# The last layer's residual: transposed by DMA during the layer in place of TensorE in the closing

## The chip, the cores and the metric

One Trainium2 chip; the kernel runs on one of its cores. The metric is device time in microseconds (us), as a median of several runs. A profile is one more execution with the hardware profiler on. It tells for each instruction when it ran and for each DMA when it landed. PE is TensorE, DVE VectorE, ACT ScalarE, POOL GpSimd, and SP the engine that here only issues DMAs. Each engine works off its own list of instructions in order, and waits where an instruction's inputs or its room are not ready.

## The reference

A trunk of two layers on 1024 tokens of 1024 channels: one layer with gated linear attention, one with chunked attention, each followed by a gated feed-forward part, and a last norm over the channels. What matters here is the end of the last layer:

```python
def conv_ffn(xn, w_up, conv_w, conv_b, w_down):
    h = causal_dwconv(xn @ w_up, conv_w) + conv_b
    gate, val = h[..., :FFN_DIM], h[..., FFN_DIM:]
    return (jax.nn.silu(gate) * val) @ w_down
...
        h = h + conv_ffn(rmsnorm(h, f_norm[layer]), f_w_up[layer], f_conv[layer], f_conv_b[layer], f_w_down[layer])
    return rmsnorm(h, final_norm)
```

All arrays are float32, and FFN_DIM is 2816. The `h` ahead of the plus sign is the residual.

## The kernel before

Activations lie with channels on the 128 partitions and tokens along the free dimension, until the last layer's end. The output wants tokens on the partitions: eight token tiles of 128 x 1024.

Every product is made of three matmuls, since each float32 operand is split in a high and a low part (`triple`). ScalarE makes the high part (a cast, L1434), GpSimd or VectorE the low part (a subtraction, L1412).

`ffn` (L1407) is the feed-forward part, called once for each layer. Its work is a list of steps, `seq`, in TensorE's order; a step is twelve matmuls of 512 columns, some 2.7 us. Beside it, `at(i, f, rank)` hangs work of the other engines on a step: in the loop at the function's end all jobs of step i are issued by rank, and then the step's matmuls. So `at` sets the place in each engine's list; when the instruction runs is up to its waits. The 22 blocks of hidden channels run through the up product (`product`), the convolution and the gate; pairs of them go through the down product (`second`). Both use a scheme of seven products for eight. `drain` copies the down product's partial sums into one of four stage buffers (L1802, ScalarE), and `send` adds these to `d_c` in DRAM by an accumulating DMA from GpSimd's queue (L1817). SP loads the up weights (`load`, L1492) and the down weights (`load_a`, L1755).

After the last down product of that scheme, whose final additions go out by `send_e` (L1824), comes the closing. `end` is the step of the last up product. The steps behind it multiply the last 512 hidden channels by their down weights (`fw`), token tile by token tile (`tile_of`, L1959): tiles 0 to 3 with three of the four blocks first, their fourth block afterwards, then tiles 4 to 7. For each tile three things are added up: these products, the sums in `d_c`, and the residual. The residual is in DRAM (`d_r1`, written at the end of attention by ScalarE's queue) with channels on the rows. `load_r` (L1948) fetches it for one token tile as two halves of four blocks of 128 channels x 128 tokens. In `tile_of`, TensorE turns each block (L1974, a transpose against the identity `ident`) into the tile's accumulator, and the products are added on top. `load_t` (L1941) fetches the sums of `d_c` into `ht`. `closing(t)` adds accumulator and `ht` on VectorE, and the last norm and the stores follow (`norm_out`).

Layer 0 begins with x in the other layout and turns it by DMA: `turn_halves` (L1280) transposes 16-bit halves of x, 256 KB each, through SBUF into a DRAM array, and later the two halves of each number are put together again by two copies (L1299).

## Time and profile before

| | |
|---|---|
| median of 3 runs | 2516.49 us (2515.58 to 2519.31) |
| profiled execution | 2516.6 us, span 2514.9 us |
| TensorE's granted clock, mean | 0.998 |
| busy: PE, DVE, ACT, POOL | 2483.2, 1835.3, 1408.7, 1496.6 us |
| DMA packets | 334.31 MB, mean 133 GB/s |

How to read the lines that follow. A group line gives source line, engine, operation, what is written and read, how often, and then durations in ns (shortest, median, longest) with the first and last start. A timeline line gives start and length in us, then the instruction; brackets tell how long the engine had been idle and what released it. The windows give the busy time of each engine between two times. The chain is followed back from the last instruction through whatever released each step. "Landing" is the time from a DMA's issue until its data are there. All times in the trace are counted from the span's start, and the closing is the stretch from about 2457 us.

### The profile page before, as it was taken

How to read it: one execution, taken by the hardware profiler on the slowest of the kernel's cores; microseconds unless marked ns; L12 is line 12 of the kernel's file. 1: busy time of each engine (PE TensorE's matmuls, PEld its weight loads, DVE VectorE, ACT ScalarE, POOL GpSimd, SP SyncE). 2: the span in 40 equal slices, each digit the busy share in tenths (PEclk: the TensorE clock that was granted, in tenths of full speed). 3: DMA queues.
4: the chain of work that ended last, by engine and by line, in shares of the span. 5: the costliest groups of instructions: out<-in, count | busy, mean ns of one | idle time of the engine just before them, and what ended most of it. 6: DMA issues, size and time to landing. Idle time of an engine off the chain costs nothing.

```text
span 2514.9 us, 39318 instructions
## 1 busy us (share of the span) xinstructions
PE 2483.2 (99%) x13905; PEld 2070.7 (82%) x13905; DVE 1835.3 (73%) x2984; ACT 1408.7 (56%) x2708; POOL 1496.6 (60%) x1523
## 2 busy tenths in 40 slices
PE   8999999999999999999999999999999999999999
PEld 6888888888878888888888888888877888888877
DVE  5765774456798888888866556667489788888884
ACT  6444555464465556565555556566456555655553
POOL 3655553357457777777635544445444777777770
PEclk9999999999999999999999999999999999999999
DMA  8743444554347777767832111122432667777795
GB/s 227 190 116 105 133 128 146 162 184 148 100 106 145 151 153 152 152 143 158 190 133 63 54 57 49 49 68 79 139 101 92 157 142 153 151 153 150 153 197 187
DMA packets 334101, 334.31 MB, mean 133 GB/s; under 512 B 50000, under 2 KB 256336, under 8 KB 333904
## 3 DMA queue, kind: packets, MB, share of 16 engines
q1 hardware_dynamic: 303232, 228.77, 31.0%
q0 software_dynamic: 25920, 94.38, 21.0%
q10 hardware_dynamic: 4752, 8.65, 1.0%
q8 instruction: 109, 1.79, 0.3%
q14 instruction: 88, 0.72, 0.1%
HBM read 180.68 MB, written 146.87 MB: 130 GB/s over the span
## 4 chain that ended last, share of the span: by engine, by line
PE 90%; POOL 3%; issue 2%; DVE 2%; ACT 1%; DMA 1%; SPq 0%; POOLq 0%; DVEq 0%; ACTq 0%
PE pu L1448 9%; PE pu L1446 9%; PE pu L1447 9%; PE acc L118 8%; PE acc L119 8%; PE acc L120 8%; PE pd L1447 4%; PE pd L1448 4%; PE pd L1446 4%; PE acco L118 2%; PE acco L120 2%; PE acco L119 2%; PE ptp L2272 2%; POOL ul L1412 1%; PE poT L2318 1%
## 5 line engine op out<-in xcount | busy, mean ns | idle before, releaser
L1412 POOL TENSOR_TENSOR ul<-r,uh 128x512 fp32r<-128x512 f32 x267 | 429.9, 1629 | 260.2 <-ACT uh L1434 255.3
L118 PE MATMUL acc<-xh,whi 128*128 128x512 f32 x896 | 374.9, 419 | 0.6 <-ACT xh L1094 0.6
L119 PE MATMUL acc<-xl,whi 128*128 128x512 f32 x896 | 352.3, 393 | 0.5 <-POOL xl L381 0.4
L120 PE MATMUL acc<-xh,wlo 128*128 128x512 f32 x896 | 351.9, 393 | 0.0
L103 POOL TENSOR_TENSOR wlo<-wraw,whi 128x256 fp32r<-128x256 f32 (+1 forms) x326 | 238.4, 761 | 140.1 <-ACT whi L101 132.8
L1434 ACT CAST uh<-r 128x512 fp32r<-128x512 f32 x289 | 177.3, 622 | 183.8 <-DVE r L1412 153.3
L1448 PE MATMUL pu<-xh,ul 128*128 128x512 f32 x524 | 204.6, 390 | 0.9 <-POOL ul L1412 0.9
L1446 PE MATMUL pu<-xh,uh 128*128 128x512 f32 x524 | 204.4, 390 | 0.7 <-ACT keep L1575 0.7
L1802 ACT COPY stage<-pd 128x1024 f32<-128x1024 f32 x180 | 175.3, 1013 | 53.0 <-PE pd L1448 51.6
L1447 PE MATMUL pu<-xl,uh 128*128 128x512 f32 x524 | 203.9, 389 | 0.0
L120 PEld LDWEIGHTS acc<-xh,wlo 128*128 128x128 f32 x896 | 168.5, 188 | 37.7
L119 PEld LDWEIGHTS acc<-xl,whi 128*128 128x128 f32 x896 | 169.6, 189 | 25.3 <-POOL xl L381 2.4
L118 PEld LDWEIGHTS acc<-xh,whi 128*128 128x128 f32 x896 | 169.3, 189 | 24.2 <-ACT xh L1094 1.0
L2227 POOL TENSOR_SCALAR sS<-sS,st 128x640 f32<-128x640 f32 (+4 forms) x128 | 86.0, 677 | 173.2 <-DVE st L2225 161.3
L1412 POOL TENSOR_TENSOR dl<-a,dh 128x512 fp32r<-128x512 f32 x90 | 151.9, 1687 | 53.6 <-ACT dh L1434 42.3
L1541 DVE SCALAR_TENSOR_TENSOR gate<-gpre,colt,gate 128x1023 f32<-128x1023 f32 (+2 forms) x92 | 173.3, 1884 | 3.2 <-ACT gate L1538 2.4
L1541 DVE SCALAR_TENSOR_TENSOR val<-vpre,colt,val 128x1023 f32<-128x1023 f32 x88 | 147.7, 1678 | 28.9 <-ACT val L1538 28.8
L2217 DVE CUSTOM_DVE_ANT_0 sS<-sc,bt 128x640 f32<-128x640 f32 (+4 forms) x128 | 84.2, 658 | 111.3 <-PE sc L2213 86.6
L1412 DVE TENSOR_TENSOR r<-r,r 128x512 f32<-128x512 f32 x160 | 130.3, 814 | 31.2 <-POOL ul L1412 30.1
L1412 DVE TENSOR_TENSOR el<-val,eh 128x512 fp32r<-128x512 f32 x90 | 86.0, 955 | 43.3 <-ACT eh L1434 43.3
L1448 PEld LDWEIGHTS pu<-xh,ul 128*128 128x128 f32 x524 | 98.3, 188 | 23.3 <-POOL ul L1412 1.8
L1446 PEld LDWEIGHTS pu<-xh,uh 128*128 128x128 f32 x524 | 98.4, 188 | 21.2 <-ACT keep L1575 1.1
(422 smaller groups left out, 7161.7 us busy)
## 6 DMA issues: line engine op xcount, KB each, us to landing
r<-in_f_w_up_dram SPq DMA_DIRECT2D x176, 256.0 KB, 4.3
d_r<-stage POOLq DMA_DIRECT2D x78, 512.0 KB, 7.9
d_c<-stage POOLq DMA_DIRECT2D x70, 512.0 KB, 8.0
a<-in_f_w_down_dram SPq DMA_DIRECT2D x72, 256.0 KB, 2.7
wraw<-in_a_w_in_dram SPq DMA_DIRECT2D x32, 512.0 KB, 4.6
d_e<-stage POOLq DMA_DIRECT2D x32, 512.0 KB, 9.2
wraw<-in_a_w_out_dram SPq DMA_DIRECT2D x16, 512.0 KB, 3.9
d_r<-h ACTq DMA_DIRECT2D x32, 256.0 KB, 2.5
```

The lines of the kernel that those rows point to most:

```text
L103: nc.gpsimd.tensor_tensor(lo[:, c], raw[:, c], hi[:, c].bitcast(F32), op=ALU.subtract)
L118: mm(ps, hi[:, kw, wcol : wcol + P], rh[k][s], start=st, stop=False)
L119: mm(ps, hi[:, kw, wcol : wcol + P], rl[k][s], start=False, stop=False)
L120: mm(ps, lo[:, kw, wcol : wcol + P], rh[k][s], start=False, stop=sp)
L1412: tt = lambda eng, o, a, b, op: eng.tensor_tensor(o, a, b, op=op)
L1434: copy(hi, src)
L1446: mm(ps, w[0][:, cw], x[0], start=first, stop=False, skip_group_check=True)
L1447: mm(ps, w[0][:, cw], x[1], start=False, stop=False, skip_group_check=True)
L1448: mm(ps, w[1][:, cw], x[0], start=False, stop=last, skip_group_check=True)
L1541: nc.vector.scalar_tensor_tensor(t_[:, a:c1], p_[:, a - step : c1 - step], w[:, 2 - step : 3 - step], t_[:, a:c1], op0=ALU.mult, op1=ALU.add)
L1802: nc.scalar.copy(t_, ps)
L2227: nc.gpsimd.tensor_scalar(S, S, st[:, 3:4], 1.0, op0=ALU.mult, op1=ALU.mult)
```

## The change

`d_r1` becomes one array of 1024 x 1024 instead of four pieces, so that a DMA can take columns out of it. From step 8 on, every third step issues one of 32 DMA transposes (`turn_r`): 512 channels x 128 sixteen-bit columns, which are 64 tokens with two halves each. Four steps later the result goes from its buffer (`rm`, two of them) back to DRAM (`put_r`, into `d_rt`). Then, in twelve rounds of five steps, quarters of the token tiles 0 to 2 are loaded (`load_r`), their halves are put together by two ScalarE copies (`join_r`), and the finished float32 rows go to `d_rj` (`send_r`). In the closing, tiles 0 to 2 of the residual are loaded whole into `ht`. For tiles 3 to 7 the halves are loaded (`load_h`) and put together there by two copies on GpSimd and two on ScalarE (`join_h`). For all eight, the sums of `d_c` are then added to `ht` by accumulating DMAs on GpSimd's queue (`add_t`). The 64 transposes on TensorE go, and so do SP's 16 loads of `d_c` and its 16 loads of residual blocks.

```diff
-    d_r1 = {(c, s): dram.tile([P, 2 * SEQ], F32, name=f"d_r1{c}{s}") for c in range(2) for s in range(2)}
+    d_r1 = dram.tile([SEQ, SEQ], F32, name="d_r1")
...
             def load_t(t):
                 fh[t] = fin.tile([P, SEQ], F32, name=f"ht{t}", tag=f"ht{t}")
-                for c in range(2):
-                    nc.sync.dma_start(out=fh[t][:, hs(c)], in_=d_c[c, t // 4, t % 4 // 2][:, hs(t % 2)])
...
-                    nc.sync.dma_start(out=r_, in_=d_r[c, t // 4].rearrange("p (f t) -> p f t", f=4)[:, :, kc[t % 4]])
-                    res[t, c] = r_
+                if t < 3:
+                    nc.sync.dma_start(out=fh[t], in_=d_rj[t])
+
+            def load_h(t):
+                for c in range(2):
...
+                    nc.sync.dma_start(out=r_, in_=d_rt[c].rearrange("(t h) c -> t h c", h=2)[t * P : (t + 1) * P])
+                    turned[t, c, 2] = r_
+
+            def join_h(t):
+                hm = fh[t].bitcast(U16).rearrange("p (t h) -> p t h", h=2)
+                for c in range(2):
+                    for i in range(2):
+                        (nc.scalar.copy if i or t < 0 else nc.gpsimd.tensor_copy)(hm[:, hs(c), i], turned[t, c, 2][:, i])
+
+            def add_t(t):
+                for c in range(2):
+                    nc.gpsimd.dma_start(out=fh[t][:, hs(c)], in_=d_c[c, t // 4, t % 4 // 2][:, hs(t % 2)], accum_op=add)
...
+            def turn_r(b, c):
+                turned[b, c] = tp.tile([P, HALF], U16, name="rm", tag="rm", bufs=2)
+                nc.sync.dma_start(out=turned[b, c], in_=rows_u[hs(c), b * P : (b + 1) * P], transpose=True)
+
+            def put_r(b, c):
+                nc.sync.dma_start(out=d_rt[c][b * P : (b + 1) * P], in_=turned[b, c])
+
+            def load_r(t, c, q):
+                r_ = parts_r[t, c, q] = tp.tile([P, 2, 256], U16, name="rm", tag="rm", bufs=2)
+                nc.sync.dma_start(out=r_, in_=d_rt[c].rearrange("(t h) c -> t h c", h=2)[t * P : (t + 1) * P, :, q * 256 : (q + 1) * 256])
+
+            def join_r(t, c, q):
+                r_ = parts_r[t, c, q]
+                f_ = parts_r[t, c, q] = tp.tile([P, 256], F32, name="rj", tag="rm", bufs=2)
+                hm = f_.bitcast(U16).rearrange("p (t h) -> p t h", h=2)
+                for i in range(2):
+                    nc.scalar.copy(hm[:, :, i], r_[:, i])
+
+            def send_r(t, c, q):
+                nc.sync.dma_start(out=d_rj[t][:, c * HALF + q * 256 : c * HALF + (q + 1) * 256], in_=parts_r[t, c, q])
...
-                            if ks[0] == 0:
-                                for f in range(n // P):
-                                    nc.tensor.matmul(ps[:, f * P : (f + 1) * P], res[t, c][:, o // P + f], ident, is_transpose=True, start=f == 0, stop=False, skip_group_check=True)
...
-                                mm(ps[:, 0:n], hh, hi, start=False, stop=False, skip_group_check=True)
+                                mm(ps[:, 0:n], hh, hi, start=k == 0, stop=False, skip_group_check=True)
...
-                at(pc[t] if t < 4 else end + 1, lambda t=t: load_r(t), 3.5)
-                at(end, lambda t=t: load_t(t), 4)
+                at(end, lambda t=t: load_t(t), 3.9)
+                if t >= 3:
+                    at(pc[t] if t < 4 else end + 1, lambda t=t: load_h(t), 3.5)
+                    at(end + 2 + t, lambda t=t: join_h(t), 4.4)
+                at(end + 2 + t, lambda t=t: add_t(t), 4.5)
                 at(pos["f", t] + 1, closing(t), 0)
+            i = 8
+            for o in range(16):
+                for c in range(2):
+                    at(i, lambda o=o, c=c: turn_r(o, c), 3.2)
+                    at(i + 4, lambda o=o, c=c: put_r(o, c), 3.2)
+                    i += 3
+            i += 3
+            for t in range(3):
+                for c in range(2):
+                    for q in range(2):
+                        at(i, lambda t=t, c=c, q=q: load_r(t, c, q), 3.2)
+                        at(i + 4, lambda t=t, c=c, q=q: join_r(t, c, q), 2.6)
+                        at(i + 5, lambda t=t, c=c, q=q: send_r(t, c, q), 3.9)
+                        i += 5
...
-                    nc.scalar.dma_start(out=quarter(d_r1, m, s), in_=h[m][:, hs(s)])
+                    nc.scalar.dma_start(out=d_r1[m * P : (m + 1) * P, hs(s)], in_=h[m][:, hs(s)])
```

GpSimd's list at the start of the closing, in the changed kernel: `fl` is the low part of the last down weights, `ht` the token tiles, `res` the loaded halves, and `d_c` the sums in DRAM.

```order
L1412 TENSOR_TENSOR fl_24944<-fr,fh_24943 128x512
L1963 DMA ht_24919<-d_c_19477 128x512
L1963 DMA ht_24919<-d_c_19481 128x512
L1963 DMA ht_24921<-d_c_19477 128x512
L1963 DMA ht_24921<-d_c_19481 128x512
L1963 DMA ht_24923<-d_c_19478 128x512
L1963 DMA ht_24923<-d_c_19482 128x512
L1959 COPY ht_24925<-res 128x512 x2
L1963 DMA ht_24925<-d_c_19478 128x512
L1963 DMA ht_24925<-d_c_19482 128x512
L1959 COPY ht_24926<-res 128x512 x2
L1963 DMA ht_24926<-d_c_19479 128x512
```

Before, the last tile's multiplication by the norm's weights (L2558) followed at once on the low part; now sixteen DMA issues and ten copies stand between. The same rows go on in this pattern up to tile 7.

ScalarE's list in the closing, in the changed kernel, from the last high part of the hidden channels on (`jk` is the square of a finished tile, `ss` its sum):

```order
L1558 CAST hidh<-val 128x512
L1959 COPY ht_24925<-res 128x512 x2
L2620 ACTIVATE jk,ss<-ht_24919 128x1024
L2622 ACT_TABLE_LOAD
L2622 ACTIVATE ss<-ss,epst 128x1
L1959 COPY ht_24926<-res 128x512 x2
L2620 ACTIVATE jk,ss<-ht_24921 128x1024
L2622 ACTIVATE ss<-ss,epst 128x1
L1959 COPY ht_24927<-res 128x512 x2
```

Tile 4's two copies (`ht_24926`) stand behind the square and the root of tile 0, tile 5's behind those of tile 1, and so on.

SP's list in the layer, in the changed kernel, where the transposes stand among weight loads (`r` up, `a` down) and the first sends of `d_c`:

```order
L1492 DMA r_20536<-in_f_w_up_dram 128x4x128
L1973 DMA_TRANSPOSE rm<-d_r_95 128x512
L1976 DMA d_rt_19540<-rm 128x512
L1815 DMA d_c_19481<-stage 128x1024
L1815 DMA d_c_19482<-stage 128x1024
L1973 DMA_TRANSPOSE rm<-d_r_95 128x512
L1976 DMA d_rt_19539<-rm 128x512
L1492 DMA r_20649<-in_f_w_up_dram 128x4x128
L1973 DMA_TRANSPOSE rm<-d_r_95 128x512
L1976 DMA d_rt_19540<-rm 128x512
L1492 DMA r_20726<-in_f_w_up_dram 128x4x128
```

Before, the rows of `DMA_TRANSPOSE` and `d_rt` were not there; the other rows stood in the same order.

More of the change, by code (lines that the diff above doesn't have):

```diff
@@ L1942, in load_t @@
                 fh[t] = fin.tile([P, SEQ], F32, name=f"ht{t}", tag=f"ht{t}")
-                for c in range(2):
-                    nc.sync.dma_start(out=fh[t][:, hs(c)], in_=d_c[c, t // 4, t % 4 // 2][:, hs(t % 2)])
-            res = {}
-            def load_r(t):
+                if t < 3:
+                    nc.sync.dma_start(out=fh[t], in_=d_rj[t])
+            def load_h(t):
                 for c in range(2):
                     if t < 4:
-                        tag = ("eh", "el", "dh", "dl")[t % 2 * 2 + c]
-                        r_ = (wd if tag[0] == "e" else wf).tile([P, 4, P], F32, name="res", tag=tag, bufs=2)
-                    else:
-                        r_ = actp.tile([P, 4, P], F32, name="res", tag=f"x{'hl'[c]}{t}_1")
-                    nc.sync.dma_start(out=r_, in_=d_r[c, t // 4].rearrange("p (f t) -> p f t", f=4)[:, :, kc[t % 4]])
-                    res[t, c] = r_
+                        r_ = (wf, wd)[t % 2 == 0].tile([P, 2, HALF], U16, name="res", tag=("eh", "el", "dh", "dl")[t % 2 * 2 + c], bufs=2)
+                    else:
+                        r_ = actp.tile([P, 2, HALF], U16, name="res", tag=f"x{'hl'[c]}{t}_1")
+                    nc.sync.dma_start(out=r_, in_=d_rt[c].rearrange("(t h) c -> t h c", h=2)[t * P : (t + 1) * P])
+                    turned[t, c, 2] = r_
@@ new lines, in join_h @@
+            def join_h(t):
[6 more added lines that the diff above has]
+                    nc.gpsimd.dma_start(out=fh[t][:, hs(c)], in_=d_c[c, t // 4, t % 4 // 2][:, hs(t % 2)], accum_op=add)
+            U16 = mybir.dt.uint16
@@ new lines, in ffn @@
+            d_rt = [dram.tile([2 * SEQ, HALF], U16, name=f"d_rt{c}") for c in range(2)]
+            d_rj = [dram.tile([P, SEQ], F32, name=f"d_rj{t}") for t in range(KT)]
+            rows_u = d_r.bitcast(U16)
+            turned, parts_r = {}, {}
+            def turn_r(b, c):
[3 more added lines that the diff above has]
+                nc.sync.dma_start(out=d_rt[c][b * P : (b + 1) * P], in_=turned[b, c])
```

## Prediction

> **What bounds the kernel now.** I read the page first, then windows over the last layer, then the chain of waits in its closing, then the closing engine by engine.
>
> From the page, the busy times and the chain by engine:
>
> ```profile
> PE 2483.2 (99%) x13905; PEld 2070.7 (82%) x13905; DVE 1835.3 (73%) x2984; ACT 1408.7 (56%) x2708; POOL 1496.6 (60%) x1523
> PE 90%; POOL 3%; issue 2%; DVE 2%; ACT 1%; DMA 1%; SPq 0%; POOLq 0%; DVEq 0%; ACTq 0%
> ```
>
> TensorE sets the time, so an edit counts by what it takes off TensorE's list or by the holes that it makes there. The windows are the stretch in which the new transposes run, that in which three tiles are put together, the rest of the layer, and the closing (us, busy of PE, PEld, DVE, ACT, POOL, then clock, DMA share, GB/s):
>
> ```profile
> 1880.00:2130.00 250.00, 247.74 (x1081) 201.50 (x1080) 212.95 (x222) 150.99 (x215) 166.32 (x115) 1.00 0.55 131
> 2130.00:2310.00 180.00, 179.97 (x791) 147.89 (x791) 152.98 (x139) 104.14 (x147) 141.43 (x106) 1.00 0.72 148
> 2310.00:2430.00 120.00, 118.95 (x521) 96.96 (x520) 101.09 (x95) 69.41 (x99) 94.11 (x72) 1.00 0.80 164
> 2430.00:2457.00 27.00, 25.82 (x116) 21.02 (x115) 20.47 (x18) 15.78 (x22) 14.51 (x10) 1.00 1.07 271
> 2457.00:2515.00 58.00, 51.58 (x268) 42.70 (x266) 28.23 (x51) 18.20 (x37) 3.13 (x2) 0.98 0.52 173
> ```
>
> PE has no holes from 2130 to 2310 (179.97 of 180); new work there can only hurt. The closing is PE too: the other engines are half idle, and the 6.4 us without PE are the last tile's norm and store. In it stand the 64 transposes, first as a group, then as pieces of the chain:
>
> ```profile
> L1974 PE MATMUL pf<-ident,res x64: 270/272/273, 2456.8 to 2506.9; 128*128 128x128 f32 x64
> ...
> 2456.93 0.44 PE pf L1974 x4
> ...
> 2459.46 0.44 PE pf L1974 x4
> ...
> 2482.70 0.44 PE pf L1974 x4
> ...
> 2485.93 0.44 PE pf L1974 x4
> ```
>
> **Removed: the transposes.** One lasts 272 ns, but they overlap: four take 0.44 us of the chain. From 2456.93 to 2459.46 is 2.53 us for four of them and nine matmuls, and nine at 0.23 are 2.1, so 0.44 is what they cost. There are 16 such fours: 7.0 us. What the end follows is VectorE's addition of the last tile's first half, so I looked at VectorE (start, length, what ended the idle time):
>
> ```profile
> 2478.53 2.69 DVE L1412 TENSOR_TENSOR ht<-pf,ht 128x512 f32<-128x512 f32 x4 [11.47 <-PE pf L1980]
> ...
> 2495.64 1.29 DVE L1412 TENSOR_TENSOR ht<-pf,ht 128x512 f32<-128x512 f32 x2 [3.22 <-PE pf L1980]
> ...
> 2502.09 0.69 DVE L1412 TENSOR_TENSOR ht<-pf,ht 128x512 f32<-128x512 f32 x1 [2.53 <-PE pf L1980]
> ...
> 2505.31 0.69 DVE L1412 TENSOR_TENSOR ht<-pf,ht 128x512 f32<-128x512 f32 x1 [1.01 <-PE pf L1980]
> ```
>
> Ahead of 2505.31 stand 15 of the fours; what follows it is VectorE's and ScalarE's own. So the end gains 15 x 0.44 = 6.6 us. VectorE keeps up: the first eight groups take 3.5 us from both, the later ones another 3.1 from PE alone, and VectorE's waits for PE after 2491 sum to over 6.7 us (3.22 + 2.53 + 1.01).
>
> The Trainium skill, "TensorE: Matmul & The Clock Gate", Part 4 (PE-mode transpose), puts a transpose at about 275 ns inside a kernel. The row's 272 agrees, but as a cost on the path it would make 64 x 0.275 = 17.6 us; the chain's 0.44 for four decides.
>
> **Added in the closing.** Tiles 0 to 2 come whole. For tiles 3 to 7 GpSimd and ScalarE each copy two halves, and for all eight GpSimd issues two accumulating DMAs, 16 in place of SP's 16 plain loads. So GpSimd, nearly idle there, becomes a chain of its own. Its prices:
>
> ```profile
> L1299 POOL COPY xs<-xm x16: 759/955/1235, 542.1 to 641.1; 128x512 uint16<-128x512 uint16 x16
> ...
> L1817 POOL DMA_DIRECT2D d_c<-stage x64: 848/900/1493, 1981.4 to 2426.7; - x64
> ...
> DMA to landing us min/median/max: 5.2/8.0/11.4
> ```
>
> ```profile
> 2461.14 1.29 POOL L1412 TENSOR_TENSOR fl<-fr,fh 128x512 fp32r<-128x512 f32 x1 [4.70 <-ACT fh L1874]
> ...
> 2465.72 0.62 ACT L1558 CAST hidh<-val 128x512 fp32r<-128x512 f32 x1 [0.76 <-DVE val L1412]
> 2479.86 1.06 ACT L2573 ACTIVATE jk<-ht 128x1024 f32<-128x1024 f32 x1 [13.52 <-DVE ht L1412]
> 2480.82 0.18 ACT L2573 ACTIVATION_READ_ACCUMULATOR jk<-ht 128x1 f32 x1
> 2481.02 1.28 ACT L2575 ACT_TABLE_LOAD   x1
> 2482.32 0.30 ACT L2575 ACTIVATE ss<-ss,epst 128x1 f32<-128x1 f32 x1
> ```
>
> ```profile
> 2452.12 11.57 SPq L1944 DMA_DIRECT2D ht<-d_c  x16
> 2463.79 7.12 SPq L1956 DMA_DIRECT2D res<-d_r  x8
> ```
>
> On SP three loads take the place of the sixteen at 2452.12, so tiles 0 to 2 are there before 2462, and the eight loads for tiles 4 to 7 start some 7 us before 2463.79 (their room comes free with PE's last product, at 2456.8): none is waited for. GpSimd is free at 2462.4. Six issues at 0.9 bring it to 2467.8, tile 3's two copies at 0.95 and two issues to 2471.5, tile 4's copies to 2473.4. There it waits: tile 4's copies on ScalarE are queued behind tile 0's square and table load. Those start 3.5 us earlier than now and end at 2479.1; with a copy at 0.6 the first half is free at 2479.7. A tile then costs GpSimd 3.7 us, so tile 7's issues start at about 2490.8 and 2491.7. An accumulating 256 KB into SBUF is not in the trace. Near rows are the 8.0 us above for twice the bytes and 5.5 for a plain 256 KB load of the same data:
>
> ```profile
> ht<-d_c SPq DMA_DIRECT2D x16, 256.0 KB, 5.5
> ```
>
> I take 6: tile 7 is whole at 2496.8 and 2497.7. VectorE wants its first half at 2505.3 - 6.6 = 2498.7. Margin 1.9 us, cost nothing; at 8.0 the margin is gone. With every length at its longest (1.235, 1.493, 8.0) tile 7 comes at 2504.1, 5.4 late; with a landing of 11.4 as well, 8.8 late, and the end is 2.2 later than now. ScalarE's u16 copies are unseen too; between its 256- and 1024-element rows (0.4 and 1.06) I take 0.6, and ten of them are hidden in its waits.
>
> **Moved: the transposes by DMA.** Layer 0 already turns x this way: 16 transfers of 256 KB against 32 of 128 KB now, the same 4.19 MB.
>
> ```profile
> L1280 SPq DMA_TRANSPOSE xm<-in_x_dram x16: 1159/1292/6231, 11.6 to 73.2; - x16
> ...
> xm<-in_x_dram SPq DMA_TRANSPOSE x16, 3.7
> ...
> q1 hardware_dynamic: 28707, 14.70, 86.4%
> ...
> q1 hardware_dynamic: 15789, 10.71, 54.7%
> ...
> L1492 SPq DMA_DIRECT2D r<-in_f_w_up_dram x176: 367/434/1437, 637.4 to 2429.9; - x176
> ```
>
> The two q1 rows are SP's queue from 10 to 80 us, with the transposes, and from 80 to 150, without. At the second's rate (38.3 us of 16 engines for 10.71 MB) the first's other 10.5 MB take 37.6 of 60.5 us; the transposes took 23. In the new place that is 23 us in 250 us, and writing 4.19 MB back another 15: the share rises from 0.55 to about 0.70, under the 0.80 that the layer bears later with one us lost. On SP a transpose holds the queue 1.3 us; a weight load behind it is late by that and by a put's wait, up to 3.7. Such loads land in some 4 us and are issued several steps of 2.7 us ahead. ScalarE's 24 small copies (0.3 to 0.4 each) stand in its list ahead of a step's casts; operands are made two steps (5.5 us) ahead, and that hides one pair of 0.8. I charge 0.5 us for all of it; bounds 0 and, with the 24 copies fully on the path, 10.
>
> **Given back.** Six of the eight residual loads that stand before the closing go. They fall where the DMA share is 1.07, GpSimd waits 5.5 us for a transfer, and PE then loses 1.19:
>
> ```profile
> 2438.29 0.86 POOL L1824 DMA_DIRECT2D d_c<-stage  x1 [5.49 <-DMA d_c<-stage]
> ...
> 2440.76 0.50 PE L1448 MATMUL pul<-xh,ul 128*128 128x512 f32 x1 [1.19 <-POOL ul L1412]
> ```
>
> I take 0.5 of that 1.19.
>
> **Sum.** The profiled execution took 2516.6 us (span 2514.9 and 1.7 around it), 0.1 over the median of 2516.49. 2516.6 - 6.6 + 0.5 - 0.5 = 2510.0.
>
> **Rivals.** *Tiles late in the closing*: GpSimd's chain passes 2498.7 and the end follows tile 7. For it: 16 issues and ten copies in a row, behind ScalarE. Against: the margin of 1.9 at median lengths. With half of the longest lateness, 2.7 us, 2512.7; with 5.4, 2515.4.
>
> *Holes in the layer*: SP, now waiting for ScalarE's copies before each reload, hands out weight loads late. Against: loads are early now. 12 rounds at 0.3 to 0.5 us make 4 to 6: 2514 to 2516.
>
> *Slower*: the transposes and their writes delay GpSimd's accumulating sends, and ScalarE's next copy into the same stage buffer waits, then PE.
>
> ```profile
> 2246.14 0.86 POOL L1817 DMA_DIRECT2D d_c<-stage  x1 [0.25 <-PE pu L1448]
> ...
> 2257.22 1.92 ACT L1802 COPY stage<-pd 128x1024 f32<-128x1024 f32 x2
> ```
>
> The send of 2246.14 must have landed when the second copy starts, 12.0 us later; landings now reach 11.4. A transpose is 23/32 = 0.7 us of all engines. From a mean lateness of 0.6 us at each of some 20 such places in five rounds of 57 us the loss passes 12 us, and the kernel is slower beyond 0.2%; at one us it is 20: 2530. Against: the median landing is 8.0 and the share only 0.70.
>
> The Trainium skill, "VectorE: DVE Perf Modes", Rules for kernel authors, advises TensorE for a 128x128 transpose where PSUM will do, and gives 1309 ns against 390 by DMA; that rule speaks for this rival. Here 256 KB, eight such blocks, land in 3.7 us, not 10.5, and off TensorE's list.
>
> That the change leaves the transposes in is excluded by TensorE's list.
>
> **Chances.** Forecast 0.55, tiles late 0.20, holes 0.13, slower 0.12. About 0.2%, 5 us, can be told from no change: faster needs 2511.5. All of the forecast and a little of the milder rivals give faster 0.57; their rest is the same, 0.30; slower 0.13. The forecast's own range is 2507.5 (both ends of the given-back and no charge) to 2512; with the rivals up to no change, 2507.0 to 2517.5.
>
> **What would show it.** Right, in the profile of the changed kernel: no PE line with ident, the closing's PE busy time about 45 us, VectorE's additions there released by PE, GpSimd's last accumulating issue some 5 us ahead of tile 7's first addition, a median landing of 5 to 7 us for those DMAs. Wrong: an addition released by an accumulating DMA (tiles late); PE idle over 1 us between 2130 and 2310, behind ScalarE's casts or a weight load (holes); stage copies released by a DMA and d_c landings well over 8.0 before 2130 (slower); a ring wait of the transposes on SP of more than 4 us, which I have not charged.

## The result and the profile after

| | before | after |
|---|---|---|
| median | 2517.09 us (2515.13 to 2520.12) | 2509.79 us (2507.95 to 2515.74) |
| ratio | | 0.9974, interval [0.9966, 0.9982] |
| profiled execution | 2516.6 us, span 2514.9 | 2515.74 us, span 2514.0 |

The change makes the kernel 7.3 us faster in this set of runs; 2510.0 was predicted. In a second set (below) the unaltered kernel came to 2513.21 beside 2517.48 for the one before, 4.3 us faster. The profiled execution of the changed kernel is the slowest of its set; TensorE's clock was halved in it for two more short stretches ahead of the last layer's feed-forward part, and the last section comes back to them.

So spans can't be compared. What can is TensorE's list: without the transposes it is the same 13,841 products in every kernel here. I took the time from the start of the 11,401st (near 1944 us, past all those stretches) to that of the 13,501st (near 2424 us), called **layer** below, and from there to the end of the span, called **closing**. The hole is TensorE's idle time ahead of one product near 2440 us, behind GpSimd's wait for a transfer, of which the prediction gave back 0.5 us; it lies within the closing. (Each of the four profiles that lack it, or have under 0.2 us of it, shows another hole of 0.15 us some 10 us later, which is not in the table.) All are worked out from one profile for each kernel:

| kernel | median us | layer us | closing us | hole us |
|---|---|---|---|---|
| before | 2517.09 | 479.95 | 90.63 | 1.19 |
| after | 2509.79 | 481.03 | 82.74 | none |
| after, second profile | 2513.21 | 481.15 | 83.62 | 1.21 |
| no PE transposes | 2507.64 | 480.12 | 83.83 | 1.30 |
| nor their loads | 2508.42 | 480.14 | 82.88 | none |
| no DMA turns | 2509.63 | 480.02 | 83.53 | 1.21 |
| no rounds | 2511.60 | 480.15 | 83.90 | 0.15 |
| turns twice | 2519.98 | 496.84 | 83.92 | 1.22 |
| no room | 2526.40 | 495.81 | 83.55 | 1.21 |
| no room, late writes | 2510.80 | 481.06 | 83.54 | 1.22 |
| all in closing | 2513.15 | 480.05 | 85.14 | 1.94 |
| early copies | 2511.75 | 481.97 | 83.53 | 1.21 |
| all in closing, early | 2513.89 | 480.00 | 84.87 | 0.17 |
| one in layer, early | 2510.67 | 480.53 | 83.40 | 1.21 |

Sums of the two parts: 570.58 before, 563.77 after, 564.77 in the second profile. The change takes 5.8 to 6.8 us off them, and the one us between is the hole. The medians are 7.3 apart in the one set and 4.3 in the other; the difference of both from the 5.8 to 6.8 lies within the spread of the runs.

The changed kernel's page, busy times and chain by engine:

```profile
PE 2481.1 (99%) x13841; PEld 2068.4 (82%) x13841; DVE 1844.0 (73%) x2984; ACT 1422.3 (57%) x2742; POOL 1521.1 (61%) x1549
PE 83%; POOL 5%; DVE 4%; issue 4%; ACT 2%; DMA 2%; SPq 0%; POOLq 0%; DVEq 0%; ACTq 0%
```

The 64 transposes are gone from PE (13905 to 13841). GpSimd's part of the chain has grown from 3% to 5%. The changed kernel's windows; the last two are cut 6.5 us later than before's, since everything there runs about that much later in this profile:

```profile
1880.00:2130.00 250.00, 247.95 (x1084) 202.29 (x1083) 214.55 (x225) 149.35 (x213) 162.10 (x113) 1.00 0.69 157
2130.00:2310.00 180.00, 179.30 (x788) 147.12 (x787) 151.52 (x141) 113.51 (x175) 141.70 (x103) 1.00 0.79 165
2310.00:2430.00 120.00, 118.72 (x520) 96.76 (x519) 102.64 (x93) 68.20 (x98) 94.24 (x73) 1.00 0.80 165
2430.00:2463.50 33.50, 33.35 (x147) 26.98 (x146) 28.84 (x24) 19.88 (x28) 19.45 (x15) 1.00 0.99 261
2463.50:2515.00 51.50, 43.98 (x203) 36.20 (x201) 30.81 (x51) 24.57 (x47) 25.77 (x28) 0.95 0.81 198
```

In the first row the DMA share has gone from 0.55 to 0.69 and TensorE has lost nothing. In the second, with the twelve rounds, ScalarE has 9.4 us more and TensorE lost 0.7 of 180. In the closing TensorE is busy for 44 us, where it was for 51.6. TensorE's timeline shows where the layer lost time:

```profile
2222.81 0.50 PE L1448 MATMUL pu<-xt2h,ul 128*128 128x512 f32 x1 [0.40 <-POOL ul L1412]
...
2280.54 0.50 PE L1448 MATMUL pu<-xt2h,ul 128*128 128x512 f32 x1 [0.27 <-POOL ul L1412]
...
2338.41 0.50 PE L1448 MATMUL pu<-xt2h,ul 128*128 128x512 f32 x1 [0.38 <-POOL ul L1412]
```

Three holes, 58 us apart, 1.05 us in sum, each behind GpSimd's low part of an up weight. Before, of these places only one had a hole, of 0.16 us.

In the closing, GpSimd's timeline:

```profile
2468.76 5.44 POOL L1963 DMA_DIRECT2D ht<-d_c  x6
...
2486.23 1.77 POOL L1963 DMA_DIRECT2D ht<-d_c  x2 [7.42 <-ACT ht L1959]
...
2489.09 2.58 POOL L1963 DMA_DIRECT2D ht<-d_c  x2
...
2496.35 2.54 POOL L1963 DMA_DIRECT2D ht<-d_c  x2
```

Six issues for tiles 0 to 2, tile 3's copies and issues between, then a wait of 7.4 us for ScalarE's copies of tile 4, and from 2489.09 to 2496.35 two tiles: 3.63 us each. That is the chain that was forecast. VectorE's additions, and the line and landing of the accumulating DMAs (ns, then us, shortest, median, longest):

```profile
2480.97 2.69 DVE L1412 TENSOR_TENSOR ht<-pf,ht 128x512 f32<-128x512 f32 x4 [7.52 <-PE pf L2010]
...
2502.09 0.69 DVE L1412 TENSOR_TENSOR ht<-pf,ht 128x512 f32<-128x512 f32 x1 [0.94 <-DMA ht<-d_c]
...
2504.73 0.69 DVE L1412 TENSOR_TENSOR ht<-pf,ht 128x512 f32<-128x512 f32 x1 [0.42 <-PE pf L2010]
```

```profile
L1963 POOL DMA_DIRECT2D ht<-d_c x16: 872/1427/2649, 2468.8 to 2497.5; - x16
...
DMA to landing us min/median/max: 3.9/7.5/9.5
```

In the timeline, tile 6's second half waited 0.94 us for its accumulating DMA; the last tile's first half (2504.73) was released by TensorE. So here the end hangs on TensorE still, but the margin is used up. In the second profile of the same kernel tile 6 waits longer:

```profile
2500.40 0.69 DVE L1412 TENSOR_TENSOR ht<-pf,ht 128x512 f32<-128x512 f32 x1 [1.31 <-DMA ht<-d_c]
...
2502.64 0.69 DVE L1412 TENSOR_TENSOR ht<-pf,ht 128x512 f32<-128x512 f32 x1
```

There VectorE comes to the last tile straight from this work, with no wait for TensorE. By the distance to TensorE's last product it is some 0.1 us late, so in that profile the end hangs on the transfer.

### The profile page after: what moved, and what is told of

Read it like the earlier page. It is cut to its first block, busy times and chain, and to the rows that moved or that the text cites. A ratio compares the mean times of both kernels' runs of the same rounds, so it can differ in the third digit from the quotient of the medians.

```text
span 2514.0 us, 39359 instructions
## 1 busy us (share of the span) xinstructions
PE 2481.1 (99%) x13841; PEld 2068.4 (82%) x13841; DVE 1844.0 (73%) x2984; ACT 1422.3 (57%) x2742; POOL 1521.1 (61%) x1549
## 4 chain that ended last, share of the span: by engine, by line
PE 83%; POOL 5%; DVE 4%; issue 4%; ACT 2%; DMA 2%; SPq 0%; POOLq 0%; DVEq 0%; ACTq 0%
PE acc L118 8%; PE acc L119 8%; PE acc L120 8%; PE pu L1448 8%; PE pu L1446 8%; PE pu L1447 8%; PE pd L1446 3%; PE pd L1448 3%; PE pd L1447 3%; POOL ul L1412 2%; PE acco L118 2%; PE acco L120 2%; PE acco L119 2%; PE ptp L2319 2%; PE poT L2365 1%
```

## The experiments

**The gain by itself.** The kernel before without the 64 transposes (the residual is left out of the output; its loads stay), and without the 16 loads too.

```diff
-                            if ks[0] == 0:
-                                for f in range(n // P):
-                                    nc.tensor.matmul(ps[:, f * P : (f + 1) * P], res[t, c][:, o // P + f], ident, is_transpose=True, ...)
...
-                at(pc[t] if t < 4 else end + 1, lambda t=t: load_r(t), 3.5)
```

The last line goes in the second of the two only.

> The kernel before with TensorE's 64 transposes taken out and nothing put in their place; the residual's loads stay, and the residual is left out of the output. If the transposes' place in TensorE's list is the gain (16 fours at 0.44 us, 15 of them ahead of the last tile's first addition): 2517.1 - 6.6 = 2510.5 us, and the hole of 1.2 us ahead of the closing stays. If the gain of the change comes from the loads that went (fewer residual loads at a full DMA share): 2515 to 2517 us here, with the closing bound by VectorE or a DMA in place of TensorE.

> As the one before, and the 16 residual loads are left out as well. If the loads ahead of the closing slow GpSimd's accumulating sends and so make the hole of 1.2 us on TensorE: 2509.3 us, no hole over 0.3 us between 2430 and 2457, and GpSimd's wait of 5.5 us for a send shorter by about one. If they cost nothing: the same as without them, 2510.5 us.

Measured: 2507.64 us (ratio 0.9965 [0.9953, 0.9978]) and 2508.42 (0.9966 [0.9953, 0.9979]). The first's closing is 83.83 us with its hole on TensorE at 1.30:

```profile
2436.84 0.50 PE L1448 MATMUL pul<-xh,ul 128*128 128x512 f32 x1 [1.30 <-POOL ul L1412]
```

Both closings without their holes: 90.63 - 1.19 = 89.44, and 83.83 - 1.30 = 82.53. So taking the transposes off is worth 6.9 us, and the changed kernel can't have more from them. In the second the hole is gone, but the second profile of the changed kernel (below) shows that this alone proves nothing for the loads. Both medians lie below what was expected. Part of that stands ahead of the layer, where the two kernels are as before: the first's profiled execution had no stretch at half clock before its end, and in both a hole of TensorE near 1850 us is 0.7 us, where every other kernel here has 2.3 to 2.4. Why was not found.

**The layer's new work taken away.** The changed kernel without transposes, writes and rounds; and with transposes and writes but without the rounds. The closing then reads as many bytes of other data instead: for tiles 0 to 2 untransposed rows of the residual, and in the first kernel for tiles 3 to 7 the halves of x. So the output lacks the right residual.

```diff
-                    at(i, lambda o=o, c=c: turn_r(o, c), 3.2)
-                    at(i + 4, lambda o=o, c=c: put_r(o, c), 3.2)
...
-                        at(i, lambda t=t, c=c, q=q: load_r(t, c, q), 3.2)
-                        at(i + 4, lambda t=t, c=c, q=q: join_r(t, c, q), 2.6)
-                        at(i + 5, lambda t=t, c=c, q=q: send_r(t, c, q), 3.9)
```

> The changed kernel without the 32 DMA transposes, their writes and the twelve rounds of putting together in the layer; the closing is whole, but reads other data of the same shape (x's halves and untransposed rows) in place of the residual, so the output lacks the right residual. If the work in the layer costs what its holes on TensorE show (0.40 + 0.27 + 0.38 in the rounds, nothing for the transposes): 2509.8 - 1.1 = 2508.7 us. If transposes or writes cost more than holes show (slower matmuls, later sends): 2506 us or less.

> The changed kernel with its 32 DMA transposes and writes, but without the twelve rounds; tiles 0 to 2 load untransposed rows in the closing, so their residual is wrong. If only the rounds make holes (ScalarE's copies ahead of its casts): the same as without transposes and rounds, 2508.7 us, and no hole over 0.15 us from 2140 to 2350. If the transposes and writes cost as well: above that one by what they cost, up to 2509.8 us if they are all of it.

Measured: 2509.63 us (0.9974 [0.9964, 0.9984]) and 2511.60 (0.9976 [0.9967, 0.9984]). Against the change's 0.9974 [0.9966, 0.9982], the times don't tell them apart. The layer does: 480.02 and 480.15 us, against 481.03 and 481.15 with all of it and 479.95 before. So the 32 transposes and their writes cost at most 0.2 us, and the rounds about 1. The three holes go with the rounds: without them only the one of 0.16 to 0.24 us that the kernel before has is left, and in the kernel without room below, where the rounds follow earlier, three such holes stand at 2007.14, 2064.89 and 2122.75, again 58 us apart.

**More transposes, and the same ones without room.** In the first, each transpose and its write is made twice, the second write into a buffer that nobody reads. In the second, there is a transpose in each step instead of each third, and its write one step behind it instead of four.

```diff
+                    at(i + 2, lambda o=o, c=c: turn_r(o, c, 1), 3.25)
+                    at(i + 4, lambda o=o, c=c: put_r(o, c, 1), 3.25)
```

```diff
-                    at(i + 4, lambda o=o, c=c: put_r(o, c), 3.2)
-                    i += 3
+                    at(i + 1, lambda o=o, c=c: put_r(o, c), 3.2)
+                    i += 1
```

> The changed kernel with each of the 32 transposing transfers, and each write of what it turned, made twice, the second pair into a buffer that nobody reads; the computation is whole. Theory (the layer has room for them: in the changed kernel's trace TensorE loses nothing in the 200 us of the transposes): the DMA engines' share between 1880 and 2130 goes from 0.69 to about 0.80, TensorE's holes there stay below 0.2 us in sum, 2509.8 to 2510.3. Rival of the prediction (transposes delay the stage sends, and ScalarE's stage copies wait for these): ScalarE's stage copies released by DMA and TensorE idle in the layer, 2515 or more.

> The changed kernel without the room between its transfers: a transpose in every step instead of every third, its write one step later instead of four; all else, the rounds' spacing too, as in the change, nothing left out. Theory (room keeps SP's queue from waiting for a transpose to land ahead of the weight loads): SP waits a landing of several us ahead of each write, 64 us and more in the same 32 steps, the weight loads behind it come late, and TensorE shows holes that VectorE's and ScalarE's weight work releases: some 2 to 10 us slower than the change, 2512 to 2520. Rival (weight loads run far enough ahead that SP's waits are covered): SP waits as long, TensorE's holes between 1880 and 2130 stay under 0.3 us, 2509.8.

Measured: 2519.98 us (1.0027 [1.0010, 1.0045]) and 2526.40 (1.0032 [1.0020, 1.0044]). My theory of the first fell: the share went to 0.80 as expected, but the layer lost 16 us in the profiled execution (its time was 2528.94; the median is 10 us above the change's). Of the kernel with doubled transposes, the window, then the largest hole of TensorE, ScalarE's cast ahead of it and SP's timeline ahead of that:

```profile
1880.00:2130.00 250.00, 244.02 (x1059) 196.89 (x1058) 208.46 (x219) 147.07 (x207) 162.26 (x112) 1.00 0.80 179
```

```profile
2163.43 0.79 PE L1446 MATMUL pu<-xh,uh 128*128 128x512 f32 x1 [5.48 <-ACT uh L1434]
...
2162.76 0.62 ACT L1434 CAST uh<-r 128x512 fp32r<-128x512 f32 x1 [10.74 <-DMA r<-in_f_w_up_dram]
...
2148.58 10.90 SPq L1975 DMA_TRANSPOSE rm<-d_r  x2
2159.52 0.58 SPq L1492 DMA_DIRECT2D r<-in_f_w_up_dram  x1
```

From 2148.58 SP took 10.9 us for two transposes, 7.0 of them waiting for their buffer (3.9 for a transpose to land in it, 3.1 for a write out of it). The weight load behind them went out at 2159.52, ScalarE waited 10.74 us for it, and TensorE 5.48. No stage copy was released by a DMA, as the rival would have it. The doubled transposes write into the same buffer as the first ones, so this kernel lengthens SP's waits too and can't tell them from crowded DMA engines.

Without room, SP waited in the same way, and what queued behind it was something else. Its waits over 1880 to 2130 for SP and for ScalarE (us in sum, times, longest), and the timelines of ScalarE, SP and TensorE near the largest hole:

```profile
SPq L1976 <- DMA rm<-d_r: 36.2, 23, 5.5
```

```profile
ACT stage L1802 <- DMA d_c<-stage: 18.2, 6, 8.8
```

```profile
1974.49 1.01 ACT L1802 COPY stage<-pd 128x1024 f32<-128x1024 f32 x1 [0.25 <-DMA d_c<-stage]
...
1982.67 0.90 SPq L1815 DMA_DIRECT2D d_c<-stage  x2
...
1986.83 1.01 ACT L1802 COPY stage<-pd 128x1024 f32<-128x1024 f32 x1 [8.76 <-DMA d_c<-stage]
...
1987.89 0.79 PE L1446 MATMUL pd<-dh,eh 128*128 128x512 f32 x1 [5.12 <-ACT stage L1802]
```

Until about 2000 us SP also sends the stage buffers (L1815). Those filled by 1975.5 went out at 1982.67, behind writes that stood for the landing of their transposes; ScalarE's next copy into these buffers waited 8.76 us, and TensorE 5.12. A second hole of 2.71 us followed at 2001.70 in the same way. The size was above my 2 to 10 us, and the work that came late was the stage copies, not the weights that I had named.

**What lack of room means.** The same dense transposes, with the writes moved behind all of them. All writes send the last two blocks, so the output lacks most of the residual.

```diff
-                nc.sync.dma_start(out=d_rt[c][b * P : (b + 1) * P], in_=turned[b, c])
+                nc.sync.dma_start(out=d_rt[c][b * P : (b + 1) * P], in_=turned[15, c])
...
-                    at(i + 4, lambda o=o, c=c: put_r(o, c), 3.2)
-                    i += 3
+                    at(41 + 2 * (2 * o + c), lambda o=o, c=c: put_r(o, c), 3.2)
+                    i += 1
+            i = 104
```

> The changed kernel with a transposing transfer in every step, as in the run without room, but with the 32 writes moved behind all of them, two steps apart; the rounds stand where the change has them. All writes then send the two last blocks, so 30 of the residual's 32 turned blocks are left out of the output, with the same bytes moved. Theory (what cost 15 us without room is SP's queue: a write one step behind its transpose waits on SP for the landing, and the stage sends and weight loads queue behind it): SP's waits for landed transposes shrink from 36 us to a few, ScalarE's stage copies are no longer released by DMA, TensorE's holes between 1915 and 2130 stay under 0.5 us in sum: 2509.8 to 2511. Rival (transposes so close together crowd the DMA engines, and stage sends land late): stage copies released by DMA with 18 us of waits as without room, 2520 or more.

Measured: 2510.80 us (0.9975 [0.9965, 0.9985]), layer 481.06. SP's waits from 1880 to 2130 and ScalarE's from 1880 to 2180, and the window from 1915 to 2005, in which the last of the dense transposes and the first writes ran:

```profile
SPq L1973 <- DMA rm<-d_r: 4.5, 6, 1.9
...
SPq L1976 <- DMA rm<-d_r: 0.3, 1, 0.3
```

```profile
ACT stage L1802 <- DMA d_c<-stage: 0.6, 1, 0.6
```

```profile
1915.00:2005.00 90.00, 90.00 (x398) 74.19 (x397) 74.30 (x78) 59.08 (x83) 58.94 (x38) 1.00 0.63 166
```

TensorE is busy all 90 us. Without room, in the same window:

```profile
1915.00:2005.00 90.00, 81.21 (x340) 65.32 (x339) 64.34 (x69) 48.37 (x68) 43.77 (x29) 0.95 0.66 178
```

The DMA share is about the same, and TensorE was busy for 81.21 us. The transposes come as densely as in the slow kernel (32 in 109 us, there in 128), and SP's stage sends land equally fast in this window (3.9 us in the median in both). So what cost 15 us is not the load on the DMA engines but SP's list: a write one step behind its transpose stands for the landing, with everything that SP has to issue behind it. This settles the second of the two kernels above; that the doubled one has the same cause follows from its rows, but wasn't tried apart.

**Where the tiles are put together.** All eight in the closing; the change with ScalarE's copies of tiles 3 to 7 ahead of tile 0's square; all eight in the closing with such early copies; and one in the layer, seven in the closing, early too.

```diff
-                if t < 3:
+                if t < 0:
...
-            for t in range(3):
+            for t in range(0):
```

```diff
-                    at(end + 2 + t, lambda t=t: join_h(t), 4.4)
+                    at(end + 2 + t, lambda t=t: join_h(t, 0), 4.4)
+                    at(end + 2 + min(t, 3), lambda t=t: join_h(t, 1), 4.4 + t / 100)
```

Here `join_h(t, 0)` makes GpSimd's two copies, `join_h(t, 1)` ScalarE's.

> The changed kernel with all eight token tiles put together in the closing, none during the layer; places and engines as in the change, nothing left out of the computation. Theory: the layer gives back the 0.9 us that the three tiles' rounds cost there (holes of 0.40, 0.27 and 0.38 us in the changed kernel's trace against 0.16 before), but GpSimd's chain of 3.65 us per tile becomes three tiles longer ahead of its wait for ScalarE, and its last accumulating transfer is issued some 3 us later, about 2499.6 instead of 2496.4; the last two tiles then come 2 to 4 us late, and VectorE's additions of tiles 6 and 7 are released by those transfers: 2509.8 - 0.9 + 3 = about 2512. Rival (the wait for ScalarE's copies ends last either way, so the three extra tiles fit into GpSimd's 7.4 us of waiting): additions of tile 7 released by TensorE, 2508.9.

> The changed kernel with ScalarE's copies of tiles 3 to 7 all placed ahead of tile 0's square, where ScalarE stands idle for 8.25 us; nothing left out. Theory (GpSimd's 7.42 us wait comes from ScalarE's order alone, and GpSimd's chain is not what ends last): GpSimd's last accumulating issue moves from 2496.4 to about 2489 to 2490 after the same start, VectorE's wait of 0.94 us for tile 6's second half is gone, and the end moves by at most 0.4 us: 2509.4 to 2509.8. Rival (the closing's end hangs on the accumulating transfers): 1 to 2 us faster, about 2508.3.

> All eight tiles put together in the closing, none in the layer, and ScalarE's copies of tiles 3 to 7 ahead of tile 0's square; nothing left out. Theory: the layer's 0.9 us comes back; ScalarE's sixteen copies take 11.2 us of 8.25 us idle time, so tile 0's square comes 1 to 2 us late, which VectorE's later idle time takes up; GpSimd's chain is eight tiles of 3.65 us from about 2470 and ends near 2499.6, some 3 us later than in the change, so the last tile comes 2 to 3 us late: 2509.8 - 0.9 + 2.5 = about 2511.4. Rival (GpSimd's copies are quicker, 2.3 us per tile, while VectorE is idle, and the chain ends by 2496): 2508.9.

> One tile put together in the layer, seven in the closing, ScalarE's copies ahead of tile 0's square; nothing left out. Theory: two thirds of the layer's 0.9 us come back, GpSimd's seven tiles end near 2496, as in the change, and tile 7 is there in time: 2509.8 - 0.6 = about 2509.2, with the additions of tile 7 released by TensorE. Rival (the layer's holes don't come from the rounds): holes of 0.3 to 0.4 us as before at the same places, and 2509.8.

Measured: 2513.15 us (0.9983 [0.9973, 0.9993]), 2511.75 (0.9981 [0.9971, 0.9990]), 2513.89 (0.9985 [0.9975, 0.9994]) and 2510.67 (0.9973 [0.9964, 0.9983]). All intervals overlap the change's; none beats it by what can be measured. (The last is 0.8 us ahead of the change in the two parts at an equal hole, 563.93 against 564.77.)

By the phases: without rounds the layer takes 480.05 and 480.00 us, with four of the twelve 480.53 (of the three holes the first, 0.42 at 2217.60, and the old one of 0.16 are left), with all 481.03 to 481.15, and 481.97 in the kernel with early copies, which has one more hole, of 0.70 us at 2337.41. So a tile put together there costs some 0.35 to 0.5 us. The early copies free GpSimd: its last issues start at 2486.85, with no wait for ScalarE ahead, and none of VectorE's additions waits for a transfer any more:

```profile
2486.85 2.54 POOL L1962 DMA_DIRECT2D ht<-d_c  x2
...
2501.78 0.69 DVE L1412 TENSOR_TENSOR ht<-pf,ht 128x512 f32<-128x512 f32 x1 [2.09 <-PE pf L2009]
```

Its closing without the hole is 83.53 - 1.21 = 82.32 us, against 82.74 in the change and 82.41 in the change's second profile. So an idle GpSimd wait of 7.4 us was worth 0.1 to 0.4 us, as the theory had it, although the median (2511.75) came out above the 2509.4 to 2509.8 expected. With all eight tiles in the closing GpSimd's chain is longer. There, with early copies, tile 6 waits for its transfers:

```profile
2496.31 0.69 DVE L1412 TENSOR_TENSOR ht<-pf,ht 128x512 f32<-128x512 f32 x1 [0.63 <-DMA ht<-d_c]
2498.31 0.69 DVE L1412 TENSOR_TENSOR ht<-pf,ht 128x512 f32<-128x512 f32 x1 [1.31 <-DMA ht<-d_c]
```

From the start of TensorE's last product to the end of the span this kernel takes 8.74 us, the change 6.80 and 6.89 in its two profiles. It gives back about 2 us for the one that it saves in the layer. Without early copies it is 7.67 us. But the kernel without rounds, whose closing does the same work as the change's, takes 7.78, with tile 6 waiting 1.21 and 1.17 us. So one us of lateness can come without the three extra tiles: what they cost is shown, at about one us more than that, for the kernel with early copies alone. In both runs with eight tiles, tile 6 is released by its transfers and VectorE comes to tile 7 without a wait for TensorE, so the rivals of these two runs, that the tiles are there in time, fell.

**The changed kernel once more**, unaltered.

> The changed kernel once more, unaltered, for a second profiled execution. Theory: what differed between the kernels' profiles because of the change stays (TensorE's holes of 0.3 to 0.4 us at the three places of the rounds' stretch, 0.9 to 1.2 us more than before in sum; GpSimd's accumulating issues at the same distances), and what was chance does not (the stretches at half clock near 533 and 1861 us). The hole of 1.2 us ahead of the closing, gone in the first profile of the changed kernel and in three of the nine experiments, there in the others: if the change removes it, it is gone again; if chance decides it (the landing of one send of GpSimd's, 4.5 us or 5.2 to 5.5), either. Time 2509.8, within 1.5.

Measured: 2513.21 us (0.9983 [0.9972, 0.9993]), outside the 1.5 us that were expected; with the first time's runs the median of all 21 is 2510.17. The same kernel's medians thus differ by 3.4 us from one set of runs to another. Its TensorE timeline:

```profile
2219.82 0.50 PE L1448 MATMUL pu<-xt2h,ul 128*128 128x512 f32 x1 [0.38 <-POOL ul L1412]
...
2277.55 0.50 PE L1448 MATMUL pu<-xt2h,ul 128*128 128x512 f32 x1 [0.24 <-POOL ul L1412]
...
2335.43 0.50 PE L1448 MATMUL pu<-xt2h,ul 128*128 128x512 f32 x1 [0.40 <-POOL ul L1412]
...
2444.87 0.50 PE L1448 MATMUL pul<-xh,ul 128*128 128x512 f32 x1 [1.21 <-POOL ul L1412]
```

The layer's three holes are there again, to within 0.03 us. The hole ahead of the closing, gone in the first profile, is back at 1.21. Over all profiles it is absent or under 0.2 us in four and at 1.2 to 1.9 in ten, among kernels with the change and without: chance takes part in it, and no run shows that the change does.

## Why the prediction was right, and where a term was off

The time was right (2510.0; 2509.79, and 2510.17 over all runs), and so was its mechanism: TensorE's list sets the time, and the transposes leave it. That it was right to 0.2 us is luck: two sets of runs of this kernel are 3.4 us apart, and of the smaller terms one was too low and one was a guess. The terms, against the two profiles of the changed kernel:

| term | predicted | measured |
|---|---|---|
| transposes off the path | -6.6 | -6.9 (the kernel before without them) |
| all new work in the layer | +0.5 | +1.1 and +1.2 |
| hole ahead of the closing given back | -0.5 | -1.2 and 0.0 |
| tiles late in the closing | 0 | -0.1 to +0.2 |
| sum | -6.6 | -6.8 and -5.8 |

The fourth row is what the closing without its hole takes more than the 82.53 us of the kernel before without transposes: 82.74 and 82.41.

*Transposes.* Fifteen fours of 0.44 us were counted as ahead of the last tile's first addition. From the start of the closing to this addition, without the hole, it is 79.89 us before and 73.02 in the kernel without transposes: 6.87 us for the fifteen, 0.46 for each four.

*Layer.* The charge was mis-sized by 0.6, and its cause was mixed: transposes and writes, which I took for the larger load, cost nothing that shows, and the rounds cost a us. Of the sign listed for "holes", TensorE idle behind ScalarE's casts, the rows show a relative: TensorE waits for GpSimd's low parts three times, 0.67 us between 2130 and 2310, less than the 1 us of the sign. Where the time is lost shows some 43 us ahead of each hole. GpSimd's low parts and VectorE's next subtractions, first before, then after:

```profile
2171.35 2.55 POOL L1412 TENSOR_TENSOR ul<-r,uh 128x512 fp32r<-128x512 f32 x2 [0.17 <-ACT uh L1434]
2174.38 0.68 DVE L1412 TENSOR_TENSOR val<-val 128x512 f32<-128x512 f32 x1
```

```profile
2177.99 3.00 POOL L1412 TENSOR_TENSOR ul<-r,uh 128x512 fp32r<-128x512 f32 x2 [0.17 <-ACT uh L1434]
2179.77 1.77 DVE L1412 TENSOR_TENSOR val<-val 128x512 f32<-128x512 f32 x1
```

Here TensorE is 5.96 us later than before, but GpSimd's low parts are 6.64 later: a round's two copies on ScalarE have put the cast ahead of them back by 0.7. So they now run beside this subtraction of VectorE, which takes 1.77 us, not 0.68. Part of VectorE's and ScalarE's work stays some 0.6 us behind from there to the hole. The profiles show such an extra slow subtraction once for each tile that is put together in the layer (three with twelve rounds, one with four; the kernel with doubled transposes has a fourth), and none without rounds. That the collision makes the hole is read from this order; it wasn't tried apart.

*Room.* The sign "a ring wait of the transposes on SP of more than 4 us" came, and harmed nothing. The changed kernel's waits of SP from 1880 to 2130:

```profile
SPq L1973 <- DMA d_rt<-rm: 79.0, 22, 14.4
```

SP runs ahead of TensorE in this kernel until it must wait for something. A long wait there cost time only where what stood behind it was due, as in the kernels without room and with doubled transposes. I listed the wait's length as the sign; the sign is who is released late.

*Given back.* Half of 1.19 was a guess between all and nothing, and the profiles show both. The term as an effect of the change isn't supported.

*Closing.* The single prices were too low: a landing of 7.5 us for 6, an issue of 1.43 for 0.9, GpSimd's copies at a median of 1.76 in the second profile for 0.95. The chain still came out at 3.63 us a tile for 3.7, since copies and issues overlap. At a landing of 8.0 the margin of 1.9 was to be gone, and at 7.5 and 7.9, the medians of the two profiles, it is: tile 6 waits 0.94 and 1.31 us. So a sign of the rival "tiles late", an addition released by an accumulating DMA, is there in both, at a price of 0 and about 0.1 us. In the kernel without rounds, which has the change's own closing and lacked the hole, it is one us, and with eight tiles in the closing 1 to 2, less than the 2.7 to 5.4 that the rival was given.

*Slower.* That rival's place (stage copies waiting for their sends) and its size (13 us and more) were right for the kernel without room. Its cause was not: sends are late because SP issues them late, not because transposes fill the DMA engines. GpSimd's sends in the changed kernel from 1975 to 2130, beside the transposes:

```profile
L1817 POOL DMA_DIRECT2D d_c<-stage x20: 857/956/1474, 1987.4 to 2126.8; - x20
...
DMA to landing us min/median/max: 5.2/8.7/13.5
```

Their median landing was 8.1 us before; it is 8.7 here and 8.2 in the second profile. The transposes may thus put them back by up to 0.6 us, the mean lateness from which the rival was to lose 12 us, but no copy into a stage buffer waited for them in the changed kernel.

*Range.* The lower end, 2507.5, does not follow from its words: with the whole 1.19 given back and no charge the sum is 2508.8.

## What to carry to other kernels

When one engine's list sets the time, price an edit by what leaves that list at the pitch of the chain (0.11 us a transpose), not at the length of one instruction (0.27). Work moved to a DMA queue cost little here by its bytes and much by what it waited for at the head of that queue: leave so many steps between a transfer and the one that needs it that the landing is over, and look at what queues behind. Gains of one us in a profile, such as a hole that vanishes, need a second profile of the same kernel before they are credited to the edit.

## What the runs showed of the hardware that I had not expected

**GpSimd's copies slow VectorE.** VectorE's pair of multiplications for the norm in the changed kernel, beside GpSimd's 16-bit copies and after them:

```profile
2488.00 2.47 DVE L2626 SCALAR_TENSOR_TENSOR ht<-ht,ss,g_fin 128x512 f32<-128x512 f32 x2
...
2498.96 1.41 DVE L2626 SCALAR_TENSOR_TENSOR ht<-ht,ss,g_fin 128x512 f32<-128x512 f32 x2
```

2.3 to 2.5 us a pair against 1.4, three times in a row, while the additions between them, which read one operand from TensorE's accumulator, keep their 1.28 a pair. The Trainium skill, "SBUF — State Buffer", Who interferes with whom, says that a VectorE instruction with two SBUF inputs contends with a GpSimd instruction that reads SBUF, and that one with at most one SBUF input outside the two-port modes does not. The trace agrees: both inputs of the slow ones lie in SBUF. With ScalarE's copies early, where GpSimd's last copies start at 2484.92, only the pair at 2485.12 is slow (3.03 us), and the six behind it take 1.4. The slowing was not charged; it took up about 3 us of VectorE's spare time in the closing. That it had a part in using up the margin isn't shown: VectorE itself stood idle for 0.94 us ahead of tile 6.

**After idle times of some 2 us TensorE's clock was halved in some executions, and in others not.** The same product in both kernels after the same hole, and the clock (the number ahead of the DMA share) in 3.4 us from some 2 us behind its end; first before, then after:

```profile
1854.25 0.94 PE L372 MATMUL pss<-ones,nacc 128*128 128x2 f32 x7 [2.35 <-DVE nacc L367]
...
1856.00:1859.40 3.40, 3.40 (x20) 2.95 (x20) 2.71 (x5) 1.85 (x5) 0.63 (x1) 1.00 1.06 291
```

```profile
1859.41 0.83 PE L372 MATMUL pss<-ones,nacc 128*128 128x2 f32 x6 [2.33 <-DVE nacc L367]
...
1861.20:1864.60 3.40, 3.40 (x14) 3.01 (x14) 2.23 (x4) 1.27 (x4) 0.06 (x1) 0.50 1.15 269
```

Holes of 2.35 and 2.33 us: full clock and 20 products after the one, half clock and 14 after the other. Over the profiles such stretches, 3.4 or 6.8 us long, appear in some and not in others at the same three places, near 605 and 1858 us after holes of 2.3 to 2.5 us and near 533 us after one or two of 1.2 to 1.9. The change touches none of them. At the start of the layer the changed kernel's profile is 6.0 us behind the other's, and some 5 of these came up near 533 and 1858 us. The large holes of the two slow kernels, 5.48, 5.12 and 2.71 us, each came with one as well, which adds to their price; the hole of 1.94 us in the kernel with all tiles in the closing did not. The Trainium skill, "TensorE: Matmul & The Clock Gate", Why this matters for your kernels, advises against idle gaps of over about 3 us between bursts of products. The rule fits the 5 us holes; here such stretches followed holes of 2.3 to 2.7 us in some executions, and near 533 us shorter ones. What decides it is not shown.
